# A hybrid retention and sliding-window layer on one core: the second value pair formed from plain operands, squares placed behind the operand sums, roots spread in three steps, one empty step more per head

## The chip, the core and the metric

The kernel runs on one core of one Trainium2 chip. A core has five engines with a queue each: TensorE (PE, matrix products into PSUM), VectorE (DVE), ScalarE (ACT), GpSimd (POOL) and SyncE (SP, which here issues most of the DMAs). Every engine works its own queue strictly in order; semaphores hold an instruction until what it reads is there and what it overwrites is free. The metric is the device time of one execution in microseconds (us), the median of the runs.

## The reference, cut to what matters

One inference step of one layer, for a prompt of 1024 tokens and a sample chunk of 64 tokens (1088 columns in all, model width 1024, float32):

```python
xn = rms_norm(x, g_attn)
rq, rk, rv, rg, sq, sk, sv, ga, gb = split(xn @ w_in)      # the projections
# A: retention, 4 heads of 256 wide; rotary embedding on rq and rk
s = einsum(q, k) * decay;  o = s @ v + (q @ state) * q_dec
state = state * gamma**C + (k * k_dec).T @ v
a = (rms_norm(o) * silu(rg)) @ w_ret_out
# B: sliding-window attention with sinks and a relative bias
b = swa_attend(sq, sk, sv) @ w_swa_out
x += (sigmoid(ga) * a + sigmoid(gb) * b) @ w_mix_out
x += cross_attn(rms_norm(x), mk, mv) @ w_co
x += (silu(rms_norm(x) @ w_gate) * (rms_norm(x) @ w_up)) @ w_down
y = rms_norm(x, g_final)
```

The kernel also returns the retention states, the window's and the memory's keys and values. All of it stays as it is; the change touches only how and when the first projections and the retention branch's steps are worked.

## The kernel before, in words

**Numbers.** Every float32 operand is split into a high part (an ACT cast, line 125) and a low part (a DVE subtraction, line 126), and a product is three matmuls: high by high, high by low, low by high (lines 209, 210, 212). Tokens lie along the columns, in two halves t of 544 columns, and inputs in two halves j of 512 rows, so that the activations xn are four quarters B11, B12, B21, B22 (512 rows by 544 tokens; the gain g_attn is multiplied in).

**A pair.** Output columns are made 256 at a time ("a pair" of weight tiles i = 0, 1). A product is one quarter of the weights by one quarter of the activations: 24 matmuls of 272 columns into one bank pair of PSUM, of which there are three ("pq"). `plain` makes a pair from eight such products; `strassen` makes it from seven, on sums of the weight quarters (`weight_ops`, lines 186 to 193: two halves of the weights are added in place, on POOL or, with `by`, on DVE; then seven casts and subtractions into five slots "wq") and on sums T1 to T4 of the activations. Three additions on DVE ("u", line 270) and one per result (line 646) put the products together. The seven products come in the order P1 (on B11), P2 (B21), P6 (T2), P5 (T1), P7 (T3), P3 (B22), P4 (T4). `plain_weights` and `plain_columns` exist in the kernel already; the latter makes a pair's eight products half of the tokens by half. A plain product's result is copied out by ACT (line 644).

**The order at the start.** `start_phase` loads the tokens and the first two pairs of w_v, forms B, and then the sums: line 486 (T1), 489 (T2), `put_sum` line 1493 (T3), 500 (T4), each followed by its casts and subtractions. `project_phase` then makes the pairs: value pair 0 (`plain`), value pair 1 (`strassen`, on weights made with `by=nc.vector`), key pair 0 (w_k), query pair 0 (w_q); then for each of the heads 1 to 3 keys, queries, values (heads 2 and 3) and window queries; then the window's keys and values, the last window queries, and the gates of A in pairs m = 0, 2, 4, 6; then the gates rg and gb.

The results of a pair go through tiles: "early" (four tiles, memory given back with `sctx.close()`) or "stage" (eight tiles that go round, in memory that held the inputs of the sums before). Keys and queries are rotated on DVE (lines 677 to 683) once both halves i are there, which needs four more of the eight stage tiles, and stored to d_qkv. Behind `sctx.close()` the pool "ra" is laid over the memory of "early", the first weights and B12: it holds the rope table, the inputs of the squares and all tiles of the retention branch.

**Squares and roots.** `token_squares` loads x again (16 loads into four tiles, "xsq"), squares on ACT (line 514) and adds on DVE (line 516). `token_roots` sums them over the rows with PE and takes the roots; `spread_roots` (lines 530 to 538) spreads them over all partitions: matmuls into a PSUM tile (512, 512 and 64 tokens), each copied by ACT.

**The side branch.** From key pair 1 on, `product` puts one step of `retention_steps` into PE's order behind every product (`self.step`). Each `yield` ends a step. The steps are: three empty ones; the roots; three more; the spreading; then per head the loads, four blocks of 256 tokens with five steps each (turn keys and values, split queries, scores "pss", state "pkv", output "po"), and the sample (turn keys and values, scores "psss", turn the last output, output). The branch's PSUM tiles are two banks. `issue_after(x)` puts the instructions that follow behind x in the queue of x's engine.

## Time and profile before

| what | value |
|---|---|
| median of 3 runs | 2233.99 us (2232.12 to 2236.03) |
| the profiled execution | 2237.74 us |
| its span, first to last instruction | 2235.7 us |
| mean granted TensorE clock | 0.989 |
| busy: PE, DVE, ACT, POOL | 2166.8, 1605.8, 881.7, 703.6 us |

How to read it: times in the profile's rows are us from the start of the span. A row of the timeline gives start, duration, engine, line, operation, output<-inputs, the shape, the count, and in brackets the idle time of that engine before it and what ended it. A row of a window gives the stretch, its length, the busy time and count of PE, PEld (weight loads), DVE, ACT and POOL, then the granted clock (1.00 is full), the share of the DMA engines and GB/s. A row of waits gives who waited for whom: us in total, times, longest. Matmuls overlap, so their starts show the pace and not their durations.

### The profile page before, as it was taken

To read this page: it belongs to the slowest core of one execution; us is meant where nothing else is said; L and a number is where in the kernel's file an instruction comes from. 1 tells how busy PE (TensorE), PEld (TensorE's weight loads), DVE (VectorE), ACT (ScalarE), POOL (GpSimd) and SP (SyncE) were. 2 spreads that over 40 slices of the span, in tenths; PEclk is the share of its full clock that TensorE was granted. 3 is DMA by queue.
4 is the path that set the end of the run, shared out by engine and by line. 5 is a ranking of instruction groups with operands and counts; after the bars stand their busy time and mean duration, and the time that the engine had idled before them with its cause. 6 is when DMAs were issued, how large, how long until landed. Compare 5 with 4: busy or idle time off the path is not lost.

```text
span 2235.7 us, 42154 instructions
## 1 busy us (share of the span) xinstructions
PE 2166.8 (97%) x16620; PEld 2117.3 (95%) x16620; DVE 1605.8 (72%) x2697; ACT 881.7 (39%) x1897; POOL 703.6 (31%) x522
## 2 busy tenths in 40 slices
PE   9899999999999999999999999999999999999987
PEld 8899999999999997889999998999999999999987
DVE  7888878667688667885455555659777776779787
ACT  6334343436444356553133333324223222335433
POOL 0223535253254112220000000015555555434561
PEclk9999999999999999999999999999999999999999
DMA  6423433344444566326443112422342333476332
GB/s 213 138 98 118 143 118 123 112 146 124 156 142 166 158 237 207 115 71 210 129 153 106 56 48 65 134 85 84 132 135 91 102 116 94 129 246 202 119 120 81
DMA packets 160456, 291.90 MB, mean 131 GB/s; under 512 B 21539, under 2 KB 89059, under 8 KB 160131
## 3 DMA queue, kind: packets, MB, share of 16 engines
q1 hardware_dynamic: 151122, 263.97, 36.8%
q0 software_dynamic: 5104, 17.44, 2.1%
q10 hardware_dynamic: 4032, 7.80, 1.0%
q8 instruction: 131, 2.15, 0.4%
q14 instruction: 67, 0.54, 0.1%
HBM read 197.99 MB, written 91.95 MB: 130 GB/s over the span
## 4 chain that ended last, share of the span: by engine, by line
PE 74%; DVE 10%; DMA 6%; POOL 3%; issue 3%; ACT 3%; SPq 0%; DVEq 0%; ACTq 0%; POOLq 0%
PE pq L209 14%; PE pq L212 14%; PE pq L210 13%; PE pd L152 7%; PE pd L153 7%; PE pd L154 7%; DVE wq L126 3%; PE pss L1100 1%; DVE T L126 1%; DMA hl<-d_op 1%; DVE B L126 1%; DMA xsq<-xT 1%; PE pout L1166 1%; ACT wq L125 1%; POOL raw L189 1%
## 5 line engine op out<-in xcount | busy, mean ns | idle before, releaser
L126 DVE TENSOR_TENSOR wq<-raw,wq 128x512 fp32r<-128x512 f32 (+1 forms) x505 | 459.7, 915 | 154.5 <-ACT wq L125 152.2
L125 ACT CAST wq<-raw 128x512 fp32r<-128x512 f32 (+1 forms) x505 | 305.2, 613 | 602.5 <-PE pq L212 248.3
L209 PE MATMUL pq<-T,wq 128*128 128x272 f32 x1832 | 505.3, 293 | 20.1 <-DVE stage L646 7.8
L210 PE MATMUL pq<-T,wq 128*128 128x272 f32 x1832 | 499.8, 289 | 0.8 <-DVE T L126 0.7
L209 PE MATMUL pq<-B,wq 128*128 128x272 f32 x1526 | 419.3, 292 | 0.5 <-DVE u L270 0.5
L210 PE MATMUL pq<-B,wq 128*128 128x272 f32 x1526 | 414.9, 289 | 0.9 <-DVE B L126 0.9
L212 PE MATMUL pq<-T,wq 128*128 128x272 f32 x1832 | 380.7, 289 | 0.8 <-DVE wq L126 0.8
L186 POOL TENSOR_TENSOR raw<-raw 128x512 f32<-128x512 f32 (+1 forms) x58 | 81.6, 1406 | 939.7 <-DVE rs_r L309 485.9
L209 PEld LDWEIGHTS pq<-T,wq 128*128 128x128 f32 x1832 | 347.6, 190 | 23.3 <-issue 9.0
L210 PEld LDWEIGHTS pq<-T,wq 128*128 128x128 f32 x1832 | 350.9, 192 | 1.5 <-DVE T L126 1.5
L212 PE MATMUL pq<-B,wq 128*128 128x272 f32 x1526 | 316.6, 288 | 0.0
L210 PEld LDWEIGHTS pq<-B,wq 128*128 128x128 f32 x1526 | 291.4, 191 | 1.3 <-DVE B L126 1.3
L209 PEld LDWEIGHTS pq<-B,wq 128*128 128x128 f32 x1526 | 288.6, 189 | 1.4 <-ACT wq L125 0.7
L212 PEld LDWEIGHTS pq<-T,wq 128*128 128x128 f32 x1832 | 286.2, 189 | 1.1 <-DVE wq L126 1.0
L212 PEld LDWEIGHTS pq<-B,wq 128*128 128x128 f32 x1526 | 237.6, 189 | 0.0
L270 DVE TENSOR_TENSOR u<-pq,u 128x544 f32<-128x544 f32 x177 | 127.0, 718 | 79.1 <-PE pq L212 78.3
L189 POOL TENSOR_TENSOR raw<-raw 128x512 f32<-128x512 f32 (+1 forms) x58 | 83.1, 1432 | 117.5 <-DVE wq L126 117.5
L646 DVE TENSOR_TENSOR stage<-pq,u 128x544 f32<-128x544 f32 x112 | 80.1, 716 | 43.0 <-PE pq L212 22.8
L1128 POOL TENSOR_TENSOR t<-t,den 128x768 f32<-128x768 f32 (+2 forms) x34 | 47.7, 1403 | 137.8 <-DVE den L1126 61.1
L193 POOL TENSOR_TENSOR raw<-raw 128x512 f32<-128x512 f32 (+1 forms) x58 | 85.6, 1476 | 16.1 <-DVE wq L126 12.5
L187 POOL TENSOR_TENSOR raw<-raw 128x512 f32<-128x512 f32 (+1 forms) x58 | 83.8, 1444 | 3.7
L1658 POOL TENSOR_TENSOR y<-u,y 128x544 f32<-128x544 f32 x38 | 62.1, 1647 | 49.7 <-DVE y L1656 29.3
(404 smaller groups left out, 4762.5 us busy)
## 6 DMA issues: line engine op xcount, KB each, us to landing
hl<-d_op SPq DMA_DIRECT2D x84, 272.0 KB, 4.0
d_op<-stage SPq DMA_DIRECT2D x44, 272.0 KB, 2.2
d_op<-ht SPq DMA_DIRECT2D x44, 272.0 KB, 4.0
raw<-w_gate SPq DMA_DIRECT2D x22, 512.0 KB, 3.5
raw<-w_up SPq DMA_DIRECT2D x22, 512.0 KB, 4.7
raw<-w_down SPq DMA_DIRECT2D x16, 512.0 KB, 3.9
d_qkv<-stage SPq DMA_DIRECT2D x28, 272.0 KB, 2.4
d_gate<-stage ACTq DMA_DIRECT2D x28, 272.0 KB, 2.5
```

What stands on the lines that cost most here:

```text
L125: self.last_cast = self.nc.scalar.copy(hi, src).ins
L126: self.last_low = self.nc.vector.tensor_tensor(out=lo, in0=src, in1=hi.bitcast(F32), op=ALU.subtract).ins
L152: mm(ps, wh, xh, start=start, stop=False)
L153: mm(ps, wh, xl, start=False, stop=False)
L154: self.last_mm = mm(ps, wl, xh, start=False, stop=stop).ins
L187: tt(out=a21, in0=a21, in1=a22, op=add)
L189: tt(out=a11, in0=a22, in1=a11, op=sub)
L193: self.last_sum = tt(out=a12, in0=a12, in1=a11, op=sub).ins
L209: mm(ps[:, c, :HC], w[:, 0, ks], x[:, 0, cs], start=start, stop=False)
L210: mm(ps[:, c, :HC], w[:, 0, ks], x[:, 1, cs], start=False, stop=False)
L212: self.last_mm = mm(ps[:, c, :HC], w[:, 1, ks], x[:, 0, c * HC:(c + 1) * HC], start=False, stop=stop).ins
L270: add = lambda out, a, b: nc.vector.tensor_tensor(out=out, in0=a, in1=b, op=ALU.add)
```

## The change

- The second value pair is made by `plain_columns` from B, with four weight splits in place of the sums and seven splits, right behind the first pair and through the tiles "early". So `sctx.close()`, and with it the pool "ra", comes behind it. The stage tiles' count starts at 4, so that they go round as before. The sums from T2 on are placed behind the last split of these four weights; before, behind the fifth of the seven.
- `token_squares` is placed behind the last cast and the last low part of the sums, on ACT and on DVE; before only on DVE.
- `spread_roots` ends a step behind each of its three copies; before, all three were one step.
- The sample's part of each head has one empty step more, between turning and scores.
- The fourth pair of gate A (m = 6) is made inside the branch's range, so that there are 119 products with steps in place of 112; the pools "op" and "mp" are opened behind it. The steps of the memory phase stay with the pairs they were with.

```diff
@@ weight_ops
-    def weight_ops(self, raws, n=512, skip=(), by=None):
+    def weight_ops(self, raws, n=512, skip=()):
...
-        tt = (by or nc.gpsimd).tensor_tensor
+        tt = nc.gpsimd.tensor_tensor
...
-        self.ready = self.last_cast, self.last_low
         self.last_sum = tt(out=a12, in0=a12, in1=a11, op=sub).ins
@@ start_phase
-            self.second = self.weight_ops(self.load_raws([io["w_v"][2 + i] for i in range(2)]), by=nc.vector)
+            self.second = self.plain_weights(self.load_raws([io["w_v"][2 + i] for i in range(2)]))
...
-        with tc.issue_after(self.ready[0]), tc.issue_after(self.ready[1]):
+        with tc.issue_after(self.last_cast), tc.issue_after(self.last_low):
             for k, (b11, b12, b21, b22) in enumerate(qs):
                 nc.vector.scalar_tensor_tensor(b22, b22, g[:, k + 4:k + 5], b12, ALU.mult, ALU.subtract)
                 self.put_op("T2", k, b22)
...
-        self.sums_done = self.last_low
+        self.sums_done = self.last_cast, self.last_low
@@ spread_roots
             self.nc.scalar.copy(self.rstd[:, c0:c0 + n], pb[:, :n])
+            yield
@@ project_phase
             values(first, 0, self.plain)
-            first = self.second
+            values(self.second, 1, self.plain_columns)
             sctx.close()
-            stage, long, count = *self.stage_tiles(), [0]
+            stage, long, count = *self.stage_tiles(), [4]
...
-                values(first, 1)
                 rotated(pair("w_k", 0), 0, 1)
-                with tc.issue_after(self.sums_done):
+                with tc.issue_after(self.sums_done[0]), tc.issue_after(self.sums_done[1]):
                     self.token_squares()
...
-                for m in (0, 2, 4):
+                for m in (0, 2, 4, 6):
                     gate_columns(1, "w_ga", AF.Sigmoid, m)
                 self.finish_side()
...
-            steps = [0, 1, 2, 2, 2, 3, 3, 2, 0]
-            for idx, w, act in ((1, "w_ga", AF.Sigmoid), (0, "w_rg", AF.Silu), (2, "w_gb", AF.Sigmoid)):
-                for m in range(6 if idx == 1 else 0, KT, 2):
+            steps = [1, 2, 2, 2, 3, 3, 2, 0]
+            for idx, w, act in ((0, "w_rg", AF.Silu), (2, "w_gb", AF.Sigmoid)):
+                for m in range(0, KT, 2):
@@ retention_steps
-        self.spread_roots()
-        yield
+        yield from self.spread_roots()
@@ retention, the sample's part
         yield
+        yield
         pss = self.bank("psss")
```

A scheduler lays out each engine's queue, so the diff alone doesn't show what moves. Three places, in the rows of the queues as they are built (line numbers of the changed kernel are one lower between lines 192 and 538):

SP's queue behind the second w_v load. "early" are the value pairs' result tiles, "dm" the decay mask, "vf" head 0's values, "xsq" the squares' inputs. Before:

```order
19 L122 DMA d_qkv<-early_124 128x544
20 L122 DMA d_qkv<-early_125 128x544
21 L122 DMA d_qkv<-early_126 128x544
22 L122 DMA d_qkv<-early_127 128x544
23 L119 DMA dm<-c_dmask 128x448
24 L119 DMA vf<-d_qkv 128x2x256
25 L119 DMA rope<-c_rope 128x2176
26 L119 DMA xsq<-xT 128x544 x4
27 L119 DMA raw<-w_k 128x1024
```

And now:

```order
21 L119 DMA raw<-w_k 128x1024 x2
22 L122 DMA d_qkv<-early_126 128x544
23 L122 DMA d_qkv<-early_127 128x544
24 L122 DMA d_qkv<-early_124 128x544
25 L122 DMA d_qkv<-early_125 128x544
26 L122 DMA d_qkv<-early_126 128x544
27 L122 DMA d_qkv<-early_127 128x544
28 L119 DMA dm<-c_dmask 128x448
29 L119 DMA vf<-d_qkv 128x2x256
30 L119 DMA rope<-c_rope 128x2176
31 L119 DMA xsq<-xT 128x544 x4
32 L119 DMA raw<-w_q 128x1024 x2
```

The w_k loads moved up between the first pair's stores, and the mask, the rope table and the squares' inputs stand behind the four stores of the second pair too.

DVE's queue at the first results of key pair 0 ("stage" and "u": results and combining additions, 678 and 679 rotations, 515 the additions of squares). Now:

```order
36 L126 TENSOR_TENSOR wq<-raw,wq 128x512 x4
37 L646 TENSOR_TENSOR stage_714<-pq,u_749 128x544
38 L126 TENSOR_TENSOR wq<-raw,wq 128x512
39 L678 TENSOR_TENSOR stage_713<-stage_714,rope 128x544
40 L269 TENSOR_TENSOR u_750<-pq,u_749 128x544
41 L679 TENSOR_TENSOR stage_714<-stage_714,rope 128x544
42 L515 TENSOR_TENSOR rstd<-rstd,xsq 128x544
43 L269 TENSOR_TENSOR u_752<-pq,u_750 128x544
44 L515 TENSOR_TENSOR rstd<-rstd,xsq 128x544 x2
45 L126 TENSOR_TENSOR wq<-raw,wq 128x512 x2
```

The first addition of squares stands behind the key pair's first result (row 37); before, nine of them stood ahead of that result, among the second value pair's. The first result of query pair 0 is the 32nd instruction behind the additions of row 44.

ACT's queue at the spreading of the roots (538, in the changed kernel 537). Before:

```order
66 L308 ACTIVATE rtok<-rs_v 64x1
67 L125 CAST wq<-raw 128x512 x3
68 L538 COPY rstd<-pb 128x512 x2
69 L538 COPY rstd<-pb 128x64
70 L125 CAST wq<-raw 128x512
```

And now:

```order
72 L125 CAST wq<-raw 128x512 x2
73 L537 COPY rstd<-pb 128x512
74 L125 CAST wq<-raw 128x512
75 L272 COPY u_1558<-pq 128x544
76 L537 COPY rstd<-pb 128x512
77 L125 CAST wq<-raw 128x512
78 L537 COPY rstd<-pb 128x64
```

The three copies, which stood together, have weight casts and the copy of a product between them, as PE's spreads have a product between them.

## The prediction

> **What bounds the kernel now.** I read the page first, then the waits of PE, then the records of PE in order of time around each wait, and last the chain of waits and the queues of DVE and SP at the places that the change touches.
>
> ```profile
> span 2235.7 us, 42154 instructions
> PE 2166.8 (97%) x16620; PEld 2117.3 (95%) x16620; DVE 1605.8 (72%) x2697; ACT 881.7 (39%) x1897; POOL 703.6 (31%) x522
> PE 74%; DVE 10%; DMA 6%; POOL 3%; issue 3%; ACT 3%; SPq 0%; DVEq 0%; ACTq 0%; POOLq 0%
> ```
>
> PE is busy for 97% of the span and holds 74% of the chain, so a change pays only where PE stands still or runs at a lower clock. The part that this change rewrites is the first 620 us. From the gates of the retention branch on, the instruction order of PE is the same in both kernels but for one or two swaps, and I take the time from there on as unchanged. These are the PE records at the two ends of each stage of the opening, and at its long waits (in brackets the idle time before the record, and what ended it):
>
> ```profile
> 33.65 0.29 PE L209 MATMUL pq<-B,wq 128*128 128x272 f32 x1
> 36.66 0.29 PE L209 MATMUL pq<-B,wq 128*128 128x272 f32 x1
> ...
> 49.66 0.39 PE L209 MATMUL pq<-T,wq 128*128 128x272 f32 x1 [3.23 <-ACT T L125]
> ...
> 64.03 0.57 PE L209 MATMUL pq<-T,wq 128*128 128x272 f32 x1 [5.67 <-DVE stage L646]
> ...
> 69.06 0.29 PE L209 MATMUL pq<-B,wq 128*128 128x272 f32 x1
> ...
> 96.96 0.36 PE L209 MATMUL pq<-T,wq 128*128 128x272 f32 x1 [0.48 <-DVE stage L646]
> 104.89 0.37 PE L209 MATMUL pq<-T,wq 128*128 128x272 f32 x1 [1.64 <-DVE stage L646]
> ...
> 114.00 0.29 PE L209 MATMUL pq<-B,wq 128*128 128x272 f32 x1
> ```
>
> 33.65 and 36.66 are the first two products of the second value pair: a product of 24 matmuls takes 3.01 us. The first key pair (w_k) begins at 69.06, and the second key pair at 114.00. The value pair's seven products should take 21.1 us and take 35.4. The two waits in brackets are 8.9 of the excess, and the granted clock (last column but two) is most of the rest:
>
> ```profile
> 51.28:54.69 3.41, 3.32 (x16) 3.00 (x15) 3.41 (x5) 1.66 (x3) 1.45 (x2) 0.50 0.09 31
> 61.52:68.35 6.83, 4.32 (x19) 4.35 (x20) 6.72 (x10) 1.17 (x2) 2.56 (x2) 0.50 0.56 185
> 63.20:101.20 38.00, 36.69 (x273) 36.43 (x274) 33.67 (x48) 14.24 (x24) 9.17 (x6) 0.93 0.49 155
> ```
>
> After each wait PE works at 0.50 for a while: 3.32 and 4.32 us of work, half of it lost, 3.8 us. The third row is for later: 48 DVE instructions in 38.0 us, 33.67 of it busy.
>
> **The change, part 1: the second value pair formed plainly.** It becomes eight products on the plain operands B in place of seven, of which four used the operand sums T. It takes away the waits for T (3.23) and for the stage tiles (5.67: the stage tiles lie on the inputs that the last sums read; the pair now goes out through the tiles "early"). It adds one product, 3.01 us. Of DVE work it removes four weight sums, three weight splits, and seven additions that combine products; four results now leave by ACT copies, and PE has a third bank pair to run on meanwhile. Its four weight splits are in DVE's queue ahead of everything else and are done by about 32 us, before 33.65. So the pair ends at 33.65 + 8 x 3.01 = 57.7, and the key pair begins there instead of at 69.06: 11.3 us earlier. The first sum T is then needed two products later, at 63.7. The DVE work ahead of it and behind it:
>
> ```profile
> 36.22 2.87 DVE L489 SCALAR_TENSOR_TENSOR xg<-xg,gains,xg 128x544 f32<-128x544 f32 x4
> 39.61 5.16 DVE L126 TENSOR_TENSOR T<-xg,T 128x544 fp32r<-128x544 f32 x8
> 54.94 3.90 DVE L500 SCALAR_TENSOR_TENSOR xg<-xg,gains 128x544 f32<-128x544 f32 x4
> ```
>
> One set of sums is 2.9 to 3.9 us, eight low parts are 5.2; three sets with their 16 low parts and the four splits are about 22 us from 28 on. All sums stand by 50 to 53 us, and the wait for T is gone.
>
> **What is late next.** All eight stores out of "early" now stand in SP's queue ahead of the loads of the mask, the rope table and the squares' inputs (xsq). The last of them waits for the copy behind the pair's last product. Before, these loads came behind the first pair in the same way (SP's own records, then four pieces of the chain of waits, and three from its later part):
>
> ```profile
> 36.56 0.33 SPq L119 DMA_DIRECT2D dm<-c_dmask  x1
> 37.54 0.42 SPq L119 DMA_DIRECT2D rope<-c_rope  x1
> 38.01 2.15 SPq L119 DMA_DIRECT2D xsq<-xT  x4
> ```
>
> ```profile
> 33.84 0.62 ACT early L644
> 34.49 2.06 DMA d_qkv<-early
> 39.42 8.91 DMA xsq<-xT
> ...
> 99.92 0.65 DVE stage L682
> 100.59 3.33 DMA d_qkv<-stage
> 104.02 0.73 DVE stage L646
> ```
>
> From the pair's end (33.65) to the last of the four first xsq (39.42 + 8.91 = 48.3) it is 14.7 us. So in the changed kernel the four squares are in at 57.7 + 14.7 = 72.4, and DVE, idle but for weight splits from about 53 to 64, can begin to add them only then. Those 14 additions now fall between the combining additions and rotations of w_k and w_q, where DVE was full already: 33.67 busy of 38.0. The last three pieces show what that does. The first result of w_q needs a stage tile of w_k, which is free when w_k's last rotation (L682) is stored, 3.33 us later. In the changed queue that first result is the 32nd DVE instruction behind the third addition of squares (done at 73.7: 72.4, a square of 0.66, an addition of 0.64). At 33.67/48 = 0.70 us each it comes at 96.1, at 38.0/48 = 0.79 each at 99.0; I take the middle, 97.6. PE has three bank pairs, so its fifth product of w_q needs the bank of the second: at 57.7 + 11 x 3.01 = 90.8. It stands 6.8 us, and as after the 5.67 wait it then works some 4.3 us at 0.50, 2.2 more: 9.0, where w_k and w_q had 0.48 + 1.64 = 2.1. Both together took 114.00 - 69.06 = 44.9 and take 51.8; the second key pair begins at 109.5 instead of 114.00. Of the 11.3 us, **4.5** are left. Bounds: with a wait no longer than now, 11.3; with the 32 instructions at 0.79 and a second store of 3.3 in the way the result comes at 102.3, PE loses 11.5 and 2.2, and nothing is left. The token roots, which read the squares, come four products into w_k 1 and have some 20 us to spare.
>
> **Part 2: roots spread in three steps.** A "step" of the retention branch is put into PE's order behind every product. These are PE's waits in that stretch, and the granted clock at five of them:
>
> ```profile
> 142.29 0.43 PE L536 MATMUL pb<-ident,rtok 64*128 64x64 f32 x2 [3.17 <-ACT rstd L538]
> ...
> 187.53 0.39 PE L152 MATMUL po<-st,qs 128*128 128x256 f32 x1 [0.90 <-DVE state L899]
> 351.33 1.09 PE L979 MATMUL pb<-ident,ret_o 128*128 128x128 f32 x4 [1.99 <-ACT ret_o L969]
> 399.22 0.36 PE L152 MATMUL pss<-qs,ks 128*128 128x256 f32 x1 [2.46 <-DVE kt L857]
> 465.18 0.45 PE L935 MATMUL psss<-qsm,vf 128*64 128x64 f32 x4 [2.32 <-DVE kvs L929]
> 520.20 0.39 PE L152 MATMUL po<-st,qs 128*128 128x256 f32 x1 [2.40 <-DVE state L899]
> ```
>
> ```profile
> 143.44:146.85 3.41, 3.41 (x17) 3.41 (x17) 3.41 (x7) 0.00 (x0) 0.00 (x0) 0.50 0.21 82
> 351.65:355.07 3.42, 3.42 (x17) 3.34 (x16) 3.38 (x7) 0.54 (x2) 3.42 (x2) 0.50 0.10 37
> 399.44:402.85 3.41, 3.41 (x17) 3.41 (x17) 3.23 (x7) 0.64 (x3) 1.46 (x1) 0.50 0.33 129
> 465.00:472.00 7.00, 6.82 (x55) 6.75 (x56) 7.00 (x11) 1.55 (x4) 4.54 (x3) 1.00 0.29 83
> 520.00:527.00 7.00, 6.80 (x56) 6.80 (x57) 4.97 (x8) 5.62 (x11) 2.96 (x2) 1.00 0.55 187
> ```
>
> There are two banks for the retention branch; the third spread waits 3.17 us until ACT has copied the first, and 3.41 us at half clock follow: 3.17 + 1.7 = **4.9**. With a product of 3.01 us behind each spread, ACT has two products' time for the first copy, and the wait goes. Bounds 0 (the copies stay behind weight casts in ACT's queue, which now surround them) and 4.9; the 6 us of cover are twice the wait, so I take 4.9.
>
> [...]
>
> **Part 3: one empty step more at each head's end, and the last gate pair inside the branch.** The empty step puts a product between the turning of the sample's keys and values and its scores; the wait of 2.32 at 465.18 is of that kind (DVE had not freed the banks), and the 1.99 at 351.33 is one step behind it. With half clock (1.7) they are 6.0. But the branch now has 117 pauses in place of 111, under 119 products in place of 112, and every step of it stands two to five products later against the key, query and value pairs. The waits inside the blocks (0.90, 2.46 with 1.7, 2.40: 7.5) go to other places, and a head's end can wait in new ones. I take half of the 6.0, **3.0**, and leave the 7.5 where they are in total. Bounds: all gone, 13.5; or two more block waits of 2.46 + 1.7, 8.3 lost. The seven products of the last pair of gate A were made before too. The pools behind the branch open later by as much, and the memory phase's first load needs a tile that the branch reads last five products, 15 us, ahead of the next pair: nothing, or one such load if that cover were gone (all loads of xsq: KB each, and the median us to landing):
>
> ```profile
> xsq<-xT SPq DMA_DIRECT2D x16, 272.0 KB, 4.0
> ```
>
>
> **The sum.** 4.5 + 4.9 + 3.0 = 12.4 us. The profiled execution took 2237.74 (its span and 2.0 around it) and would take 2225.3; it lies 3.75 above the median of 2233.99, which would become **2222**.
>
> **Rivals.** (1) Nothing is given back in w_q: DVE catches up, since it has 4 + 3 + 7 instructions of 0.70 less to do, 9.8 us. Then 11.3 + 4.9 + 6.0 = 22.2 us, 2212. For it speaks the 11 us hole of DVE before 64; against it that nothing of the squares can fill this hole. (2) DVE takes all of it back (slower xsq loads, more waiting in its queue): 0 + 4.9 + 0, 2229. For it speaks 8.91 us for four xsq. (3) The spreading doesn't do what it says, ACT's copies stay late: 4.5 + 0 + 3.0 = 7.5, 2226.5. (4) The other side: the blocks meet DVE's rotations. Head 1's first block now turns its keys behind the second product of a value pair and scores behind the fourth, just as head 2's second block did where PE waited at 399.22. Each such wait costs 2.46 + 1.7 = 4.2. Parts 1 and 2 together are 9.4, so from three more on nothing is won, and four make it 7.4 slower: 2241. Against it: of 16 blocks, two cost over 2 us. (5) Short waits carry no clock with them, so that ending them gives only themselves: 4.5 + 3.2 + 2.2 = 9.9, 2224; the row at 351.65 speaks against it.
>
> **How the numbers follow.** Forecast 0.43, own range 2215 to 2228; (1) 0.17; (2) 0.20; (3) 0.08; (4) 0.09; (5) 0.03. A measurement of this kernel tells about 0.2%, 4.5 us, from no change: faster is below 2229.5, slower above 2238.5. Faster: the forecast, (1), (5), most of (3) and half of (2), 0.78; within 0.2% the other half of (2) and some of (3), 0.13; slower (4), 0.09. The range reaches from beyond (1) to beyond (2): 2209 to 2233.
>
> **What would show it.** Right: no PE wait from 33 to 58, w_k at about 57.7, rope and xsq issued at 61 to 64, a PE wait of 5 to 8 us at the fifth product of w_q with half clock behind it, the second key pair at about 109.5; no wait at L536; none at psss. Wrong: a wait for T, or a DVE queue that is done with w_k's rotations by 92; or waits for kt or state of over 2 us in more than three blocks, which would undo the gain.

## The result, and the profile after

The changed kernel takes **2218.56 us** (median of 4, 2216.99 to 2220.54); the kernel before takes 2235.01 (median of 4, 2232.12 to 2238.05). The ratio is **0.9924, 95% interval 0.9909 to 0.9939**: faster by 16.5 us, where 12 were predicted. The profiled execution took 2217.95 us, 19.8 less than the one of before. (The ratio of the two medians is 0.9926.)

From the page of the changed kernel, the span and the busy time of each engine:

```profile
span 2216.1 us, 42178 instructions
PE 2160.3 (97%) x16644; PEld 2110.2 (95%) x16644; DVE 1593.7 (72%) x2683; ACT 882.3 (40%) x1899; POOL 714.7 (32%) x522
```

Nothing of this tells where 16 us went. The stages do. Here are the stretches of the program with the busy time of each engine (after the length: PE, PE's weight loads, DVE, ACT, POOL; the last columns are the granted clock, the DMA share and GB/s). First the changed kernel, cut at the first key pair, the second key pair and the end of the retention branch; then the kernel before, cut at the same points:

```profile
25.00:57.40 32.40, 32.40 (x260) 32.40 (x259) 26.72 (x38) 19.02 (x34) 11.62 (x4) 1.00 0.25 94
57.40:102.90 45.50, 43.01 (x338) 42.37 (x337) 36.02 (x51) 19.86 (x33) 10.32 (x7) 1.00 0.65 217
102.90:601.00 498.10, 491.88 (x3884) 480.73 (x3883) 388.69 (x704) 212.57 (x448) 188.72 (x161) 1.00 0.39 126
```

```profile
25.00:69.06 44.06, 34.24 (x236) 32.87 (x235) 39.09 (x57) 23.47 (x42) 5.50 (x4) 0.88 0.44 150
69.06:114.00 44.94, 42.82 (x338) 42.34 (x337) 37.22 (x52) 15.37 (x27) 11.26 (x7) 1.00 0.44 140
114.00:621.95 507.95, 494.43 (x3886) 485.12 (x3885) 387.93 (x700) 211.18 (x446) 187.56 (x160) 0.99 0.39 127
```

The value pair lost its waits and its half clock (granted 1.00, before 0.88): PE is busy for all of 32.40 us where it was busy for 34.24 of 44.06. The first key and query pair take 45.50 instead of 44.94: the prediction had 51.8 there. The branch takes 498.4 instead of 508.0 (its last row above ends 0.4 us early); what stands behind it takes 1614.8 and 1613.7 (table below). So the gain is 11.1 us in the opening and 9.5 us in the branch, and 1.1 us are lost behind it, in these two executions.

PE's records at the ends of these stages, and the one long wait among them:

```profile
33.31 0.29 PE L208 MATMUL pq<-B,wq 128*128 128x272 f32 x1
...
57.41 0.29 PE L208 MATMUL pq<-B,wq 128*128 128x272 f32 x1
...
93.40 0.40 PE L208 MATMUL pq<-T,wq 128*128 128x272 f32 x1 [2.36 <-DVE u L269]
...
102.92 0.29 PE L208 MATMUL pq<-B,wq 128*128 128x272 f32 x1
```

The pair starts at 33.31, w_k at 57.41, the second key pair at 102.92. The wait in w_q is 2.36 us and ends with an addition (L269, u), not with a first result (L646, stage). Now DVE and SP at the places that the prediction spoke of:

```profile
68.71 0.72 DVE L678 TENSOR_TENSOR stage<-stage,rope 128x544 f32<-128x544 f32 x1 [3.69 <-DMA rope<-c_rope]
...
71.98 1.55 DVE L515 TENSOR_TENSOR rstd<-rstd,xsq 128x544 f32<-128x544 f32 x2
...
92.64 0.71 DVE L269 TENSOR_TENSOR u<-pq,u 128x544 f32<-128x544 f32 x1
...
96.64 0.71 DVE L646 TENSOR_TENSOR stage<-pq,u 128x544 f32<-128x544 f32 x1
```

```profile
60.36 0.33 SPq L119 DMA_DIRECT2D dm<-c_dmask  x1
...
61.26 0.42 SPq L119 DMA_DIRECT2D rope<-c_rope  x1
61.73 2.88 SPq L119 DMA_DIRECT2D xsq<-xT  x4
```

The rope table and the squares' inputs are issued at 61.3 to 64.6, the third addition of squares ends at 73.5, the first result of w_q begins at 96.64. All of that is as forecast. The waits of PE that the changed kernel has from 25 us to the end of the branch (in total, times, longest; four of 0.3 to 0.8 are left out):

```profile
PE pq L208 <- DVE u L269: 2.4, 1, 2.4
PE pss L152 <- DVE kt L855: 2.2, 4, 1.1
PE pq L208 <- DVE stage L646: 2.0, 2, 1.0
...
```

Of the long waits of the branch before (3.17, 1.99, 2.46, 2.32, 2.40) none is left, nor has one of over 1.2 us come for them.

### The profile page after: what moved, and what is told of

Its sections match the earlier page's. It is cut to its first block, busy times and chain, and to the rows that moved or that the text cites. A ratio compares the mean times of both kernels' runs of the same rounds, so it can differ in the third digit from the quotient of the medians.

```text
span 2216.1 us, 42178 instructions
## 1 busy us (share of the span) xinstructions
PE 2160.3 (97%) x16644; PEld 2110.2 (95%) x16644; DVE 1593.7 (72%) x2683; ACT 882.3 (40%) x1899; POOL 714.7 (32%) x522
## 4 chain that ended last, share of the span: by engine, by line
PE 75%; DVE 11%; DMA 5%; issue 3%; ACT 2%; POOL 2%; SPq 0%; POOLq 0%; DVEq 0%; ACTq 0%
PE pq L208 14%; PE pq L211 14%; PE pq L209 14%; PE pd L152 7%; PE pd L153 7%; PE pd L154 7%; DVE wq L126 3%; DMA raw<-w_down 1%; PE pss L1099 1%; PE pout L1165 1%; ACT wq L125 1%; DVE stage L646 1%; DVE T L126 1%; POOL raw L189 1%; PE pp L1142 1%
## 5 line engine op out<-in xcount | busy, mean ns | idle before, releaser
L126 DVE TENSOR_TENSOR wq<-raw,wq 128x512 fp32r<-128x512 f32 (+1 forms) x502 | 453.7, 908 | 159.3 <-ACT wq L125 156.7
L208 PE MATMUL pq<-T,wq 128*128 128x272 f32 x1800 | 494.3, 292 | 12.9 <-ACT wq L125 6.9
L209 PE MATMUL pq<-T,wq 128*128 128x272 f32 x1800 | 488.5, 288 | 0.0
L208 PE MATMUL pq<-B,wq 128*128 128x272 f32 x1550 | 424.4, 292 | 1.2 <-DVE stage L646 1.0
L209 PE MATMUL pq<-B,wq 128*128 128x272 f32 x1550 | 420.0, 288 | 0.2 <-DVE B L126 0.2
L186 POOL TENSOR_TENSOR raw<-raw 128x512 f32<-128x512 f32 (+1 forms) x58 | 85.2, 1470 | 931.3 <-DVE rs_r L308 486.0
L211 PE MATMUL pq<-T,wq 128*128 128x272 f32 x1800 | 372.7, 288 | 2.4 <-DVE wq L126 2.4
L208 PEld LDWEIGHTS pq<-T,wq 128*128 128x128 f32 x1800 | 339.4, 189 | 16.2 <-ACT wq L125 7.8
L209 PEld LDWEIGHTS pq<-T,wq 128*128 128x128 f32 x1800 | 342.9, 190 | 0.0
L211 PE MATMUL pq<-B,wq 128*128 128x272 f32 x1550 | 320.3, 287 | 0.0
L209 PEld LDWEIGHTS pq<-B,wq 128*128 128x128 f32 x1550 | 294.4, 190 | 0.5 <-DVE B L126 0.4
L208 PEld LDWEIGHTS pq<-B,wq 128*128 128x128 f32 x1550 | 291.5, 188 | 2.8 <-ACT wq L125 1.2
L211 PEld LDWEIGHTS pq<-T,wq 128*128 128x128 f32 x1800 | 279.4, 188 | 2.8 <-DVE wq L126 2.6
L211 PEld LDWEIGHTS pq<-B,wq 128*128 128x128 f32 x1550 | 240.2, 188 | 0.0
L269 DVE TENSOR_TENSOR u<-pq,u 128x544 f32<-128x544 f32 x174 | 124.8, 718 | 80.8 <-PE pq L211 80.3
L189 POOL TENSOR_TENSOR raw<-raw 128x512 f32<-128x512 f32 (+1 forms) x58 | 84.6, 1459 | 112.2 <-DVE wq L126 108.0
L646 DVE TENSOR_TENSOR stage<-pq,u 128x544 f32<-128x544 f32 x108 | 77.3, 716 | 32.7 <-PE pq L211 25.8
L192 POOL TENSOR_TENSOR raw<-raw 128x512 f32<-128x512 f32 (+1 forms) x58 | 87.8, 1514 | 15.7 <-DVE wq L126 12.2
L187 POOL TENSOR_TENSOR raw<-raw 128x512 f32<-128x512 f32 (+1 forms) x58 | 85.5, 1475 | 3.7
```

The costliest lines, as they stand in the source:

```text
L126: self.last_low = self.nc.vector.tensor_tensor(out=lo, in0=src, in1=hi.bitcast(F32), op=ALU.subtract).ins
L189: tt(out=a11, in0=a22, in1=a11, op=sub)
L192: self.last_sum = tt(out=a12, in0=a12, in1=a11, op=sub).ins
L208: mm(ps[:, c, :HC], w[:, 0, ks], x[:, 0, cs], start=start, stop=False)
L209: mm(ps[:, c, :HC], w[:, 0, ks], x[:, 1, cs], start=False, stop=False)
L211: self.last_mm = mm(ps[:, c, :HC], w[:, 1, ks], x[:, 0, c * HC:(c + 1) * HC], start=False, stop=stop).ins
```

## Experiments

All kernels of one set ran on one chip beside the kernel before, whose median there was 2234.67 (part 1, part 2, part 3, parts 2 and 3), 2232.8 (the second profiles of part 1 and of the kernel before, the fixed round, fewer squares) and 2234.15 (the other four).

**Part 1 alone.** The first part of the diff, on the kernel before:

```diff
-            self.second = self.weight_ops(self.load_raws([io["w_v"][2 + i] for i in range(2)]), by=nc.vector)
+            self.second = self.plain_weights(self.load_raws([io["w_v"][2 + i] for i in range(2)]))
...
+            values(self.second, 1, self.plain_columns)
             sctx.close()
-            stage, long, count = *self.stage_tiles(), [0]
+            stage, long, count = *self.stage_tiles(), [4]
...
-                values(first, 1)
```

> The kernel before with part 1 alone: the second value pair formed plainly, the operand sums and the squares moved behind it; roots, head ends and gate pairs as before. Theory A (the pair's gain is kept, because the fifth product of the first query pair takes the bank that the third product's addition frees; it waits 2 to 3 us and no half clock follows): second key pair at about 103 us instead of 114, 11 us gained, 2224. Rival B (the prediction's step: the query pair gives 6 to 7 us back): second key pair at 109 to 110, 4.5 us gained, 2230.5. Rival C (the parts are not additive; the early pair pays only with the other parts): the waits of the retention branch grow by what the opening won, 2230 or more.

2229.89 us (10 runs), ratio 0.9974 (0.9963 to 0.9985). The second key pair begins at 102.97 in its profile. The same kernel again, for a second profile:

> Part 1 alone once more, for a second profile (the first took 2.7 us less than its median). Theory A with D: the second key pair again at 103 within 1.5 us, a wait of 2 to 3 us at the first query pair's fifth product, and one or two half-clock stretches more or fewer in the branch (1.7 us each). Rival B: the opening itself varies, and the second key pair comes at 106 or later in this execution.

2225.18 us (one run); the second key pair at 104.17. PE's records at the two waits, first profile and second:

```profile
93.16 0.40 PE L208 MATMUL pq<-T,wq 128*128 128x272 f32 x1 [2.37 <-DVE u L269]
...
452.98 0.45 PE L933 MATMUL psss<-qsm,vf 128*64 128x64 f32 x4 [3.85 <-DVE kvs L927]
```

```profile
93.49 0.57 PE L208 MATMUL pq<-T,wq 128*128 128x272 f32 x1 [2.36 <-DVE u L269]
...
449.94 0.69 PE L933 MATMUL psss<-qsm,vf 128*64 128x64 f32 x4 [3.59 <-DVE kvs L927]
```

Rival B, the give-back in w_q, falls: twice the opening keeps 8 to 11 us and the wait is 2.4. In the second profile half clock followed it (a matmul of 0.57 in place of 0.40), in the first not. Rival C, that the branch loses what the opening won, is not seen in the profiles: the sample's wait is longer (3.85 and 3.59, before 2.32 and 2.48), but the branch as a whole takes 508.64 and 504.48 us, before 507.95 and 504.72. By the medians the part gains only 4.8 us, though, which is the time that rivals B and C named, and by the profiles about 10; see behind the table below for what is known of that.

**The kernel before, again.**

> The kernel before once more, unchanged, for a second profile. Its first profile took 3 us more than its median, and the pair alone gained 10.6 us between profiles but 4.8 us between medians. Theory D (the waits of about 2 us are the same in every execution, but whether half clock follows is left to where they fall in the clock's grid of 3.41 us): the waits at the third spread, the sample's scores and the blocks come again within 0.5 us, and of the three half-clock stretches between 140 and 410 us one or two are at other places or gone; the second key pair at 114 within 2 us. Rival E: the half clocks come again behind the same waits, and the 3 us lie behind 620 us.

2235.46 us (one run); the second key pair at 112.50. Its long waits in the branch:

```profile
139.34 0.43 PE L536 MATMUL pb<-ident,rtok 64*128 64x64 f32 x2 [1.72 <-ACT rstd L538]
...
348.08 0.84 PE L979 MATMUL pb<-ident,ret_o 128*128 128x128 f32 x4 [1.78 <-ACT ret_o L969]
393.81 0.35 PE L152 MATMUL pss<-qs,ks 128*128 128x256 f32 x1 [1.78 <-DVE kt L857]
458.43 0.45 PE L935 MATMUL psss<-qsm,vf 128*64 128x64 f32 x4 [2.48 <-DVE kvs L929]
513.99 0.39 PE L152 MATMUL po<-st,qs 128*128 128x256 f32 x1 [2.95 <-DVE state L899]
```

The same five waits are there, four of them within 0.7 us and the spreading's 1.5 us shorter. Half clock now lies behind the first and the last of them (0.52 from 139.77 to 143.18 and from 515.23 to 518.64); in the first profile it lay behind the first three (0.50 from 143.44, 351.65 and 399.44). Theory D holds in its main point: the waits recur at the same places and the half clock does not. Their sizes vary more than its 0.5 us, which only two of the five keep.

**Parts 2 and 3 together.** The changed kernel with the second value pair as before.

> The changed kernel with the second value pair as before (seven products with operand sums), so parts 2 and 3 together. Theory A: the change's 16.5 us less the 11 of the pair, 5.5 us gained, 2229.5; by the two profiles (8 us between the second key pair and the end of the branch) up to 8, 2227. Rival B: if the pair alone gives 4.5, parts 2 and 3 together must give 12, 2223.

2225.57 us (6 runs), ratio 0.9954 (0.9938 to 0.9970): 9.1 us gained, between the two theories and above the 7.9 that the prediction gave these parts. Taken together with part 1 alone (4.8), the sum is 13.9 against 16.5. By the ratios it is 5.8 + 10.3 = 16.1, against 17.0 and, on another chip, 15.0 for the whole change: within the intervals the two halves add up.

**Part 2 alone.** In both this and the next run the fourth pair of gate A is inside the branch too.

```diff
             self.nc.scalar.copy(self.rstd[:, c0:c0 + n], pb[:, :n])
+            yield
...
-        self.spread_roots()
-        yield
+        yield from self.spread_roots()
```

> The kernel before with part 2 alone: the roots spread in three steps, and the fourth pair of gate A inside the branch, since there are two steps more. Prediction: 4.9 us gained, 2230. By the trace of the changed kernel (new waits of 0.4 and 1.0 us at the spreading): about 2.4 us there, 2232.5; the head ends keep their waits of 2 us or have others, since every step of the branch stands two products later: plus or minus 3. Rival: no gain at all, 2235, if the copies of the spread roots stay late on ACT.

2226.53 us (5 runs), ratio 0.9959 (0.9944 to 0.9974): 8.1 us, more than any expectation.

**Part 3 alone.**

```diff
         yield
+        yield
         pss = self.bank("psss")
```

> The kernel before with part 3 alone: one empty step more at each head's end, and the fourth pair of gate A inside the branch. Prediction: 3 us gained, 2232; bounds 13.5 gained and 8.3 lost. The wait ahead of the spreading's last piece (3.2 us and half clock behind it) stays. If the empty step itself does it, the 2.3 us wait at the sample's scores goes and 2 to 6 us are gained; if only the place of the steps against the key and query pairs does it, the waits inside the blocks change as well and the sum may have either sign.

2226.35 us (6 runs), ratio 0.9958 (0.9942 to 0.9973): 8.3 us. Each of the two parts gains the same 8 us, and both together 9. So they do not each remove waits of their own; the gain of one is for the most part that of the other. What they have in common is that the branch's later steps stand at other products. That was tried next.

**The steps moved, the spreading undivided.** This kernel has the same order on PE as part 2 alone, but for the three pieces of the spreading, which stand together:

```diff
         self.spread_roots()
-        yield
+        for i in range(3):
+            yield
```

> The kernel before with the fourth pair of gate A inside the branch, the roots spread in one step as before, and two empty steps behind it: every later step of the branch stands where it stood with the roots spread in three steps, and only the spreading itself is undivided. Theory F (the place of the branch's steps against the key, query and value pairs decides, not the spreading): the wait of 2 to 3 us ahead of the third spread stays, with or without half clock behind it; the waits of about 2 us behind 300 us (turned results, scores, outputs, sample's scores) are gone as in the run with three steps; 5 to 6 us gained of that run's 8, 2229. Rival: the spreading gives most of the 8 us by itself, and this run gains at most 2.

2225.96 us (9 runs), ratio 0.9963 (0.9951 to 0.9975): as much as with the spreading. And nothing but the gate pair:

> The kernel before with nothing but the fourth pair of gate A moved inside the branch's range. All theories: the steps stand where they stood, so all waits up to 620 us come again, and the time is that of the kernel before within 0.2 percent. Rival G: the move itself is worth something (pools opened later, the memory phase's loads), 2 us or more of either sign, and then the runs of parts 2 and 3 each carry it.

2233.17 us (12 runs), ratio 0.9999 (0.9988 to 1.0009): no gain. PE's waits from the second key pair to the end of the branch, first with the gate pair alone, then with the steps moved by two:

```profile
PE po L152 <- DVE state L899: 4.2, 2, 2.9
PE pss L152 <- DVE kt L857: 2.7, 1, 2.7
PE psss L935 <- DVE kvs L929: 2.5, 1, 2.5
PE pb L536 <- ACT rstd L538: 2.4, 1, 2.4
PE pb L979 <- ACT ret_o L969: 2.2, 1, 2.2
```

```profile
PE pss L152 <- DVE kt L858: 1.3, 3, 0.6
PE pb L980 <- ACT ret_o L970: 1.1, 1, 1.1
PE pb L980 <- DVE sf L884: 1.1, 1, 1.1
PE po L152 <- DVE state L900: 0.8, 1, 0.8
PE pb L536 <- ACT rstd L538: 0.4, 1, 0.4
...
```

Theory F holds in its main point. Two empty steps behind the spreading take away the waits for state (2.9), keys (2.7) and the sample (2.5) and halve that for the turned results (2.2). The wait at the spreading itself is 0.4 in this execution, against the expectation that it stays. PE came to it later: half clock from 127.7 to 131.1 lay ahead of it (told at the end).

Why the place matters can be read from DVE's rows. In the kernel before, DVE stands still ahead of three results of pairs until a store has given a stage tile back:

```profile
396.33 0.72 DVE L646 TENSOR_TENSOR stage<-pq,u 128x544 f32<-128x544 f32 x1 [3.45 <-DMA d_qkv<-stage]
...
460.70 0.72 DVE L646 TENSOR_TENSOR stage<-pq,u 128x544 f32<-128x544 f32 x1 [5.44 <-DMA d_sq<-stage]
...
517.59 0.72 DVE L646 TENSOR_TENSOR stage<-pq,u 128x544 f32<-128x544 f32 x1 [4.49 <-DMA d_sq<-stage]
```

Behind each of them in DVE's queue stands work of the branch: keys (397.57), the sample (464.66) and state (519.46), and PE waits for it at 399.22, 465.18 and 520.20. With the steps moved by two, the keys of that block (395.85) and the state (511.88) stand ahead of the next result (398.29 and 515.26), and the sample (460.24) behind a result (459.61) that waits for no store. In each of the five profiles with the old places of the steps, DVE waits twice for a store to d_sq, 9.9 to 11.8 us together; in the four with moved steps and the old opening it never does, and in the two of the changed kernel at most 1.3 us. Why the stores are in time then was not followed further. The turned results waited likewise, through ACT, for a DVE instruction (L316, 350.53) behind a rotation. The wait at the spreading is another: ACT's copies (141.66) stood behind weight casts (140.62) that had waited 5.30 us for POOL's sums.

**Three bank pairs in a fixed round.** The changed kernel, with the bank pair of each product in the projecting phase set by its number and not by what comes free:

```diff
     def bank_pair(self):
-        return self.ps.tile([P, 2, 512], F32, tag="q", name="pq")
+        if self.bank_no is None:
+            return self.ps.tile([P, 2, 512], F32, tag="q", name="pq")
+        self.bank_no += 1
+        return self.ps.tile([P, 2, 512], F32, tag=f"q{self.bank_no % 3}", bufs=1, name="pq")
```

> The changed kernel with three bank pairs that are taken in a fixed round in the whole projecting phase, so that the fifth product of a pair must wait for the second product's bank, as the prediction had it. If the prediction's step was right but for the bank: PE waits at the first query pair's fifth product until the first result is out, 5 to 6 us in place of 2.4, with half clock behind it in most executions, and the second key pair begins 3 to 6 us later than 103; the whole 3 us or more slower than the changed kernel's 2218.6, since other pairs wait the same way. If the DVE queue were not the reason for the wait: no longer wait there, and 103 as before.

2221.31 us (4 runs), ratio 0.9939 (0.9915 to 0.9963), not told from the changed kernel by time alone. PE's two waits in the opening:

```profile
93.12 0.59 PE L212 MATMUL pq<-B,wq 128*128 128x272 f32 x1 [2.17 <-DVE u L273]
...
109.11 0.57 PE L212 MATMUL pq<-B,wq 128*128 128x272 f32 x1 [5.12 <-DVE stage L651]
```

With the second product's bank the fifth product came so late that the scheduler put it behind the sixth and seventh. PE now waits 2.17 ahead of the sixth, and 5.12 ahead of the second key pair, whose first product takes the postponed product's bank. Each is followed by half clock (a matmul of 0.59 and of 0.57 in place of 0.40). The second key pair begins at 109.11, and the prediction had 109.5. So the bank is what the forecast of the opening hung on, though the loss comes by another route than it named, and that the number agrees so closely is in part luck.

**Fewer squares.**

```diff
-            for k in range(KT):
+            for k in range(2):
```

> The changed kernel with two squares of each half in place of eight; twelve squares with their loads and additions are left out, so the token norms and all that hangs on them are not the reference's. Theory A: the wait of 2.4 us at the first query pair's fifth product goes (12 additions of 0.65 us are out of DVE's queue), the second key pair at about 100.5, and the rest as in the changed kernel. Rival: the wait stays, because the store out of the stage tile or the rotations hold DVE, not the squares.

2209.31 us (one run, of a kernel that leaves out most of the squares). There is no wait in w_q, and the second key pair begins at 100.33. PE's longest wait from there to the end of the branch is 0.8 us. So the squares make the 2.36, by the place that they take in DVE's queue or by what goes with them (their loads and ACT's squaring are left out too); and the 2.0 for stage tiles and 2.2 for keys that the changed kernel still has shrink as well (0.5 and 0.7).

**The changed kernel, again,** on the chip of the last set:

> The changed kernel once more, timed beside the others on the same chip, with a second profile: 2218 to 2220 us, 15 to 17 less than before. Theory A: the second key pair at 103 within 1.5 us, the wait of 2 to 3 us at the first query pair's fifth product (with half clock behind it or not), and no wait over 1.5 us from there to 600 us.

2217.46 us (6 runs), ratio 0.9933 (0.9917 to 0.9948); the second key pair at 103.79; no half clock from 25 us to the end of the branch, as in the first profile.

**The second pair's stores from POOL's queue,** an attempt at a faster version:

```diff
-            def values(w, h, by=self.strassen):
+            def values(w, h, by=self.strassen, store=self.store):
                 def emit(i, t, ps, sb):
-                    self.store(self.d_qkv[2, 2 * h + i, :, half(t)], taken(ps, sb))
+                    store(self.d_qkv[2, 2 * h + i, :, half(t)], taken(ps, sb))
...
-            values(self.second, 1, self.plain_columns)
+            values(self.second, 1, self.plain_columns, nc.gpsimd.dma_start)
```

> The changed kernel with the second value pair's four stores issued from POOL's queue, so that the mask, the rope table and the squares' inputs no longer stand behind them in SP's queue. Theory A: what its tiles allow of the rope table and the squares' inputs lands up to 8 us earlier, DVE's wait of 3.7 us for the rope table goes, the squares' additions come earlier against the first query pair, and the wait of 2.4 us at its fifth product shrinks or goes: 1 to 4 us faster than the changed kernel. Rival: POOL, whose weight sums now stand behind the stores, gives the sums of the first key pair late, and the first key pair waits: 1 to 5 us slower than it. With the tiles still bound to the second pair's stores: no difference.

2220.93 us (6 runs), ratio 0.9948 (0.9933 to 0.9963): the median is 3.5 us above the changed kernel's of the same set, and the two intervals overlap. SP issues the mask no earlier (60.89 against 60.36), and in w_q PE waits for weights (the first of two such waits):

```profile
86.30 0.40 PE L208 MATMUL pq<-T,wq 128*128 128x272 f32 x1 [1.65 <-ACT wq L125]
```

The stores are out of SP's queue, so what holds the mask is not their place there; by the third expectation it is the tiles, which lie over "early" and so wait for the second pair's stores, and that was not tested further. PE's two waits for w_q's weights, 1.6 us each, and 6.83 us at half clock from 87.14 on are what the first query pair lost. No kernel here that does all the work beats the changed one.

**All profiles by stage.** The opening ends at the first product of the second key pair, the branch at the 12,000th matmul record from the end. Idle and half clock are the sums of PE's idle time before its records, and of the stretches at 0.50, in that stage; in us:

| kernel | opening ends | branch takes | the rest | branch idle | branch at half clock |
|---|---|---|---|---|---|
| before | 114.00 | 507.95 | 1613.70 | 13.5 | 10.2 |
| before, again | 112.50 | 504.72 | 1616.35 | 11.8 | 6.8 |
| gate pair only | 112.01 | 507.07 | 1614.59 | 14.2 | 6.8 |
| part 1 | 102.97 | 508.64 | 1613.23 | 15.1 | 6.8 |
| part 1, again | 104.17 | 504.48 | 1614.71 | 11.9 | 6.8 |
| part 2 | 112.90 | 494.27 | 1617.08 | 3.6 | 0 |
| steps moved | 112.39 | 497.56 | 1615.57 | 5.2 | 3.4 |
| part 3 | 113.41 | 497.84 | 1613.02 | 6.2 | 3.4 |
| parts 2 and 3 | 111.48 | 493.65 | 1615.18 | 3.2 | 0 |
| changed | 102.92 | 498.44 | 1614.79 | 6.2 | 0 |
| changed, again | 103.79 | 497.90 | 1615.33 | 5.9 | 0 |
| fewer squares | 100.33 | 493.96 | 1613.22 | 2.8 | 0 |
| fixed round of banks | 109.11 | 495.97 | 1615.17 | 3.1 | 4.5 |
| stores on POOL | 106.03 | 497.59 | 1613.59 | 5.0 | 3.4 |

The opening is 112.7 in the mean of the seven without part 1 and 103.5 in the four with it (part 1 and the changed kernel, twice each): **9.2 us**. The branch is 506.6 in the mean of the five where its steps stand as before, 495.8 in the four where they stand elsewhere: **10.7 us**. In the changed kernel the branch is 498.2, **2.3 us** more; with fewer squares it is 493.96, in one execution. So it seems that the squares, late by part 1, give something back in the branch too, besides the 2.4 us in w_q that are in the opening already. With the old places of the steps part 1 costs the branch nothing (506.6 with and without it). 9.2 + 10.7 - 2.3 = 17.6, against 16.5 and 16.7 by the two pairs of medians.

What stays open: by its two profiles and the two of the kernel before, part 1 alone gains 8.3 to 11.0 us in the opening, but 4.8 us between medians (by the ratio 5.8, from 3.4 to 8.3 us). Its two profiled executions are among the faster of its eleven. Five of its ten executions of the first set show a mean clock of 0.989 (2228.8 to 2232.2 us), the profiled ones 0.990 and 0.991, and by estimate a thousandth less is 2.2 us more (0.001 x 2230). Part of the difference is thus likely half clock; which waits it followed in the executions without a profile cannot be seen.

## Why the prediction was right, and where it was not

The time came out 3.4 us below the forecast of 2222, inside its own range. But the sum came near with terms that were not right. The opening was put at 4.5 us and gave 9.2; this is the missing gain. Parts 2 and 3 were put at 4.9 + 3.0 = 7.9 and gave 8.4 in the branch (10.7 - 2.3). That these two agree is luck: what the 4.9 stood for, the dividing, gives nothing measurable, and what the 3.0 stood for gives nearly all.

- **The pair's end.** Predicted 57.7, measured 57.41. No wait between 33 and 58. Right.
- **What is late next.** Squares' inputs issued at 61 to 64, third addition at 73.7, first result of w_q at 96.1 to 99.0: measured 61.7, 73.5, 96.64. Right, from rows of the profile before alone.
- **The step that failed: "its fifth product of w_q needs the bank of the second".** It takes the bank that comes free first. That is the third product's: its addition (L269) runs at 92.64, the second product's reader (L646) only at 96.64. The queue shows it, since DVE's rows of w_q stand in this order (third product's addition, fourth's, then the second's first result):

```
69 L269 TENSOR_TENSOR u_1044<-pq,u_1043 128x544
...
73 L269 TENSOR_TENSOR u_1046<-pq,u_1044 128x544
74 L646 TENSOR_TENSOR stage_714<-pq,u_1043 128x544
```

  So the wait was 2.36 and not 6.8, and in three of four profiles no half clock came with it: 2.4 in place of 9.0, and the opening kept 9 to 11 us and not 4.5. With the banks in a fixed round the second key pair did come at 109.1. Rival (1) was right on the opening, but not for its reason: DVE did not catch up, PE did not need it to. In the kernel before the step was true: PE's 1.64 at 104.89, which the prediction shows, is the wait of the fifth product of w_q, and it ends with the second product's reader, since there that reader (104.02) stood ahead of the third product's addition (104.66). The change turned the two round, and the prediction took the old order over.
- **Part 2, 4.9 us.** The wait at the third spread is 3.17, 1.72, 2.41, 2.82 and 1.85 in the five profiles with the old places of the steps, with half clock behind the 3.17 (0.50) and the 1.72 (0.52) and none behind the 2.41 (a matmul of 0.40, then 0.29); with the spreading divided it is gone, as predicted. But undivided it is also only 0.4 with the steps moved and 0.2 with part 3 alone, where half clock lay ahead of it; and the kernel with the steps moved and the spreading undivided takes 2225.96, the one with it divided 2226.53. The dividing itself is worth nothing that the times can tell, with intervals of some 3 us to each side.
- **Part 3, 3.0 us, and "the 7.5 stay in total".** The failing step here is that the waits would only move on. The waits inside the blocks and at the head ends hang on how the steps stand against the pairs' results on DVE (three by its waits for stores, as shown above), and a step or two further all of them are short at once: the branch's idle time falls from between 11.8 and 15.1 to between 3.2 and 6.2, and its half clock from 6.8 or more to 3.4 or none. Either added wait of part 2 or of part 3 does it, and the second adds about 1 us. Part 3 alone gave 8.3, halfway between the 3.0 and its bound of 13.5; taking half of the 6.0 had no row behind it. Later by two steps (part 2), by one more at each head (part 3) or by both, the steps stand better; that no new long wait came with any of these places is measured, but why is shown only for the three waits above.
- **Rival (4), block waits that meet DVE's rotations,** was the same mechanism with the other sign. In the changed kernel the longest such wait is 1.1 us. **Rival (5)**: of waits of 1.7 to 3 us some carry half clock and some do not, in the same kernel at the same place (2.36 with and 2.37 without in the two profiles of part 1), so neither 1.7 a wait nor 0 is right.

## What to carry to other kernels

Where tiles come from a pool that hands out what is free first, follow the readers in their queue's order, not the order of the program, to say which one the next user waits for. Where steps of one piece of work are interleaved with another by count, try their place by itself (an empty step adds no instruction) before crediting the edit that moved them. And run the parts of an edit apart: here two parts that each gain 8 us gain 9 together.

## What the runs showed of the hardware

**Half clock, and PE's idle time ahead of it.** In the profile before, half clock begins at 51.28, 61.52, 143.44, 351.65, 399.44, 839.76, 850.00 and 2147.06: 0, 3, 27, 88, 102, 231, 234 and 614 times 3.413 us behind the first, and each of these stretches is 3.41 or 6.83 long. In the changed kernel it begins at 829.62, 1495.22 and 2126.69: 0, 195 and 380 times 3.413. Both profiles were cut into windows on these grids, from 33 to 2190 us. 25 windows at full clock have 1.2 us or more of idle PE. The 11 with 1.81 to 3.41 us are each followed by half clock, the 14 with 1.64 or less are not. Here is the same wait in two executions, part 1 again and the changed kernel again (window, its length, busy time of PE and the other engines, and the clock in the last column but two):

```profile
90.14:93.55 3.41, 1.05 (x9) 0.83 (x8) 3.41 (x7) 1.31 (x2) 0.00 (x0) 1.00 0.89 252
93.55:96.96 3.41, 3.41 (x15) 3.41 (x16) 2.61 (x5) 1.14 (x2) 0.00 (x0) 0.50 1.03 407
```

```profile
89.12:92.53 3.41, 1.69 (x14) 1.47 (x12) 3.41 (x7) 0.66 (x1) 0.00 (x0) 1.00 0.91 237
92.53:95.95 3.42, 2.77 (x22) 2.77 (x23) 1.86 (x3) 0.99 (x2) 0.00 (x0) 1.00 0.96 363
```

The wait is 2.36 in the one and 2.37 in the other. In the first it lies in one window (3.41 - 1.05 = 2.36 idle) and the next runs at 0.50; in the second the grid cuts it in two (1.72 and 0.65), and the clock stays. So in these executions it was not the length of the wait that told the two apart, but how the grid cut it. Counted by waits in the profiles before and changed: of 7 from 1.2 to 1.64 us none had half clock in it or behind it, of 12 from 1.99 to 3.23 six had, and the four of 4.38 to 6.13 all had. At 0.50 matmuls begin 0.227 us apart (before, 143.56 to 146.28), at 1.00 0.125 (24 in 3.01): a stretch of 3.41 us costs 1.5 us where PE has work, against the 1.7 that the prediction takes from the clock alone. Half clock that follows such waits in one execution and not in the next would fit the spread of the times: the kernel before, with five waits of 1.7 to 3.2 us in its branch, runs from 2226 to 2241 us and the changed one from 2215 to 2222, though in fewer runs. The executions without a profile cannot show it.

**Half clock behind 18 small matmuls.** With the steps moved, PE has no idle time at all in the window ahead of a half-clock stretch, but the 18 matmuls of the token roots, each with two columns, stand in it:

```profile
124.44 2.05 PE L525 MATMUL pt<-ones,rstd 128*128 128x2 f32 x18
```

```profile
124.29:127.70 3.41, 3.41 (x31) 3.38 (x30) 3.25 (x6) 0.00 (x0) 0.04 (x1) 1.00 0.80 245
127.70:131.11 3.41, 3.41 (x17) 3.41 (x17) 1.93 (x3) 1.95 (x3) 2.52 (x2) 0.50 0.03 8
```

Those 2.05 us lie in one window and the next is at 0.50. So it is in two other profiles: with part 3 alone the 18 matmuls begin at 125.46 and the products' matmuls last 0.43 in place of 0.29 from 127.74 on; with the stores on POOL they begin at 118.09, and matmuls last 0.43 from 121.31 on. The 3.41 us ahead of each hold them whole. In the profiles before and changed the grid cuts the 18 in two (126.06 to 128.11 at 126.37, 115.10 to 117.15 at 116.23), with at most 1.74 us of them in one window, and the clock stays at 1.00. So in these five profiles half clock came where one window held all 2.05 us of them, though PE counts as busy there, and not where the grid cut them. That their size is the reason was not shown: it was not tried with matmuls of other sizes. The half clock from 127.70 to 131.11 is the one that lay ahead of the spreading whose wait is 0.4.
